# Slots of a state-space stage dealt out anew, and side work held back while loads are played

## The chip, the cores and the metric

The kernel runs on one core of one Trainium2 chip. The metric is the device time of one execution in microseconds (us), the median of several. A core has five engines with instruction streams of their own: TensorE (PE, with its weight loads shown as PEld), VectorE (DVE), ScalarE (ACT), GpSimd (POOL) and SyncE (SP), which here only issues DMAs. 16 DMA engines carry out what SP and POOL issue.

## What is computed

Two layers of an encoder trunk on 256 tokens of width 2048, in float32. Cut to what matters:

```
h = rms_norm(x, norm_mix_g[layer])
...
x = x + mixer_conv_diff(h, ...)      # layer 0: GLU, conv, differential attention
x = x + mixer_s5(h, ...)             # layer 1: state-space layer
...
x = x + memory_cross_attention(rms_norm(x, ..), rms_norm(mem, ..), wq, wk, wv, wo)
x = x + conv_ffn(rms_norm(x, ..), w_up, dw, db, w_down)
...
# mixer_s5, per direction
bu = einsum("sgc,gpc->sgp", u, bb)   # bb from discretised parameters
h  = associative_scan(a, bu)         # over the 256 tokens, 128 groups, 64 states
y  = einsum("sgp,gcp->sgc", h, c)    # both directions summed
...
g = gelu(y + d_skip * xn);  out = (g @ w_val) * sigmoid(g @ w_gate)
```

## The kernel before

**Weights.** Every product with a weight matrix goes through tiles of 128 x 1024 float32 (512 KB), 960 in all. `wtile` (L212) loads one on SP's queue (`raw`, L217, four buffers), casts it on ScalarE to a reduced high part (`hi`, L223), and subtracts on VectorE to get the low part (`lo`, L225); `lin_ws` (L263, L264) and `lin_xs` (L298) multiply high by high, high by low and low by high. The stages follow one another: GLU and attention projections, attention, output projection (`ab_w_out`), cross-attention (`xa_wq`, `xa_wo`), FFN up and down, the state-space layer, cross-attention and FFN of layer 1. The order of the instructions on each engine is fixed when the kernel is built, by a scheduler with its own model of time; on the chip each engine works through its row in that order, and waits where a buffer or an operand isn't there.

**Side work.** What the state-space layer needs of its parameters (W1, W2, the tables d_t) is computed in pieces during layer 0. Generators stand in `self.side`; after each weight tile `background` (L228) adds the stage's rate (`RATE`, L32) to a credit and plays pieces until it is used up. `s5_w1` makes W1 in 32 blocks of 512 KB: for each, six VectorE operations on 128 x 512 (L865, 0.6 credits each), a load on SP (L873, s_b) and eight on POOL (L872, d_pw) into one of two buffers, and a write on SP (L892, d_w). The load for the block after next goes into the buffer that is being written, so it waits in SP's queue for that write. `self.loads` holds loads that are played one per weight tile (`load_one`, L573): the residual x in the first GLU tiles, and before each pair of attention heads of cross-attention their keys and values (`kvraw`, L578), which share the buffers of `raw` and are split by a cast on ScalarE (L310) and a subtraction on VectorE (L311).

**The state-space stage.** `s5` works in large slots named A0, A1, B0, B1 and B2. At its start the residual X is written to DRAM (d_x, L999) as FFN down finishes it, and read back rearranged (xc, L1003, slot A1). `rr` (L1035) holds each token's norm, xg = xc * rr * gain (L1039, eight VectorE operations) goes to B1, and TensorE transposes it (L1045, ps_u) to U in B0. Then eight blocks follow: products of U with a block of W1 (L1058, ps_sa; W1's blocks come in quads, w1s, 2 MB in four loads on POOL, L1022, here numbered 0 to 7, so that W1's second block is block 1), transposes of the result (L1069, ps_st), copies to the state (st). The matrix products of the memory's values and keys for layer 1 (`mem_kv(1)`, weights xa_wv and xa_wk) are set among all this as filling for TensorE. The scans, the state history (hprev), the products with W2 (w2r, on POOL, L1118) and tables (tq, L1120), and gT follow in the same slots.

Of the kernel before, what the change touches and what calls it, by code (L numbers as in the profile page):

```python
# [12 lines left out]
F32 = mybir.dt.float32  # L13
F32R = mybir.dt.float32r
# [8 lines left out]
NTOK = 256  # L23
# [5 lines left out]
RMS_EPS = 1e-6  # L29
LN_EPS = 1e-5  # L30
MAGIC = 12582912.0
RATE = {"glu": 1.2, "qkv": 1.29, "kv": 0.95, "out": 0.8, "wq": .7, "wo": .8, "up": .75, "down": 0.96}  # L32


class Build:
# [177 lines left out]
    def wtile(self, src):  # L213
        nc = self.nc
        part = lambda t: t.rearrange("p (k f) -> p k f", k=src.shape[1])
        raw = part(self.W.tile([128, 1024], F32, tag="raw", name="raw", bufs=4))
        dma = (nc.sync if self.begun else nc.scalar).dma_start(raw, src)  # L217
        self.begun = True
        if self.loads:
            with self.tc.issue_after(dma.ins):  # L220
                self.load_one()
        hi = part(self.W.tile([128, 1024], F32R, tag="hi", name="hi"))
        nc.scalar.copy(hi, raw)  # L223
        lo = part(self.W.tile([128, 1024], F32R, tag="lo", name="lo"))
        ins = nc.vector.tensor_tensor(lo, raw, hi.bitcast(F32), op=ALU.subtract)  # L225
        self.background(ins.ins, dma.ins)
        return hi, lo

    def background(self, ins, dma):
# [129 lines left out]
    def mixer0(self):  # L359
# [10 lines left out]

        self.rate = RATE["glu"]
        self.side.append(self.s5_params())
# [48 lines left out]

        self.rate = RATE["qkv"]
        av = S.tile([128, 2, 2048], F32, tag="B0", name="av")
# [72 lines left out]

        self.rate = RATE["kv"]
        self.side.append(self.s5_w1())
# [7 lines left out]
        cat = lambda kt: (bo[:, 0, kt], bo[:, 1, kt]) if kt < 8 else (ao[:, 0, kt - 8], ao[:, 1, kt - 8])  # L506
        self.rate = RATE["out"]
        w = a["ab_w_out"]
# [73 lines left out]
    def xattn(self, layer):  # L582
# [5 lines left out]
        ov = lambda kt, j: oT[kt // 8][:, j, kt % 8, :]  # L588
        self.rate = RATE["wq"]

# [7 lines left out]
        for h in range(XH):  # L598
# [35 lines left out]
            if h < 2:  # L634
                self.load_head(h + 2)
        self.rate = RATE["wo"]
        for n in range(4):
# [373 lines left out]
    def s5(self):  # L1011
        nc, a, M, S, R = self.nc, self.a, self.M, self.S, self.R
# [4 lines left out]
        quads = []  # L1017

        def load_quad(b):
            t = S.tile([128, 4, 4, 256], F32, tag=("A0", "B2", "A0", "B2", "B1", "B2", "B1", "B2")[b], name="w1s")  # L1020
            for i in range(4):
                nc.gpsimd.dma_start(t[:, i], self.d_w1[b * 4 + i].rearrange("p g r d -> p g (r d)"))  # L1022
            quads.append(t)

        for b in range(2):
            load_quad(b)
        xc = S.tile([128, 8, 512], F32, tag="A1", name="xc")
        self.fetch_xc(xc)
        rr = M.tile([128, 8], F32, name="rr")
# [7 lines left out]
        gc = lambda ap: ap.rearrange("p (g c) -> p g c", c=16)  # L1037
        for t in range(8):
            nc.vector.scalar_tensor_tensor(xg[:, :, 7 - t, :], gc(xc[:, t]), rr[:, t : t + 1], gc(gq), op0=ALU.mult, op1=ALU.mult)  # L1039
        U = S.tile([128, 32, 128], F32, tag="B0", name="U")  # L1040
        for b in range(8):
            ps = self.pst("ps_u")
            for i in range(4):
                gi = b * 4 + i
                nc.tensor.transpose(ps[:, i * 128 : i * 128 + 128], xg[:, gi], self.ident)  # L1045
            (nc.scalar.copy if b % 2 else nc.vector.tensor_copy)(U[:, b * 4 : b * 4 + 4], ps.rearrange("p (i x) -> p i x", i=4))
        self.dump("U", U)
        ST = []
        for b in range(8):
            hf = b // 4  # L1050
            if b % 4 == 0:
                st = S.tile([128, 2, 32, 64], F32, tag=f"A{1 - hf}", name="st")
                ST.append(st)
            pss = [self.pst("ps_sa") for _ in range(2)]
            for i in range(4):
                gi = b * 4 + i
                for q in range(4):
                    nc.tensor.matmul(pss[i // 2][q * 32 : q * 32 + 32, i % 2 * 256 : i % 2 * 256 + 256], lhsT=U[:, gi, q * 32 : q * 32 + 32], rhs=quads[b][:, i, q, :], start=True, stop=True, tile_position=(0, q * 32))  # L1058
            if b < 6:
                load_quad(b + 2)  # L1060
            for h in range(2):
                g2 = b % 4 * 2 + h
                sb = M.tile([128, 2, 512], F32, tag="y", name="sb", bufs=2)[:, 0]
                nc.scalar.copy(sb, pss[h])
                p2 = self.pst("ps_st")
                for i in range(2):
                    for j in range(2):
                        o = j * 256 + i * 128
                        nc.tensor.transpose(p2[:, o : o + 128], sb[:, i * 256 + j * 128 : i * 256 + j * 128 + 128], self.ident)  # L1069
                s4 = p2.rearrange("p (r g k) -> p r g k", r=2, g=8)  # L1070
                d4 = st[:, :, :, g2 * 8 : g2 * 8 + 8].rearrange("p r k g -> p r g k")
                nc.vector.tensor_copy(d4[0:64], s4[0:64])
                nc.scalar.copy(d4[64:128, :, :, ::-1], s4[64:128])
        ring = S.tile([128, 4, 1024], F32, tag="B2", name="w2r")
        gT, hps = [], []

        def scan(hf):
            st = ST[hf]
            gs = slice(hf * 64, hf * 64 + 64)
            Ar = self.A8[:, 0:1, gs].broadcast_to([128, 2, 64])  # L1080
            Ai = self.A8[:, 1:3, gs]
            for k in range(1, 32):
                m1 = M.tile([128, 2, 64], F32, tag="m1", name="m1", bufs=2)
                m2 = M.tile([128, 2, 64], F32, tag="m2", name="m2", bufs=2)
                nc.vector.tensor_tensor(m1, Ar, st[:, :, k - 1, :], op=ALU.mult)
                nc.vector.tensor_tensor(m2, Ai, st[:, ::-1, k - 1, :], op=ALU.mult)
                nc.vector.tensor_tensor(m1, m1, m2, op=ALU.add)
                nc.vector.tensor_tensor(st[:, :, k, :], st[:, :, k, :], m1, op=ALU.add)
            self.dump(f"st{hf}", st)
            hp = S.tile([128, 2, 64, 32], F32, tag=f"B{1 + hf}", name="hprev")  # L1090
            nc.vector.memset(hp[0:64, :, :, 0:1], 0.0)
            nc.vector.memset(hp[64:128, :, :, 31:32], 0.0)
            for g in (slice(0, 16), slice(16, 32), slice(32, 64)):
                for j in range(2):
                    hv = st[:, j, :, g].rearrange("p k g -> p g k")
                    nc.scalar.copy(hp[0:64, j, g, 1:32], hv[0:64, :, 0:31])
                    nc.vector.tensor_copy(hp[64:128, j, g, 0:31], hv[64:128, :, 30::-1])
            hps.append(hp)

        def outside(hf):  # L1100
            hp = hps[hf]
            gt = S.tile([128, 2, 2, 4, NTOK], F32R, tag=f"A{1 - hf}", name="gT")
            gT.append(gt)
            if hf:
                late = S.tile([128, 4, 1024], F32, tag="B1", name="w2r")
                more = [S.tile([128, 2, 1024], F32, tag=f"x2{i}", name="w2r") for i in range(4)]
                slots = [late[:, i] for i in range(4)] + [more[i // 2][:, i % 2] for i in range(8)]
            else:
                slots = [ring[:, i] for i in range(4)]
            for g8 in range(2):  # L1110
                yt = M.tile([128, 8, 8, 16], F32, tag="y", name="yt", bufs=2)
                for b in range(2):
                    ps = self.pst("ps_y")
                    for i in range(4):
# [8 lines left out]
                        for q in range(4):  # L1123
                            nc.tensor.matmul(o[q], lhsT=U[:, gi, q * 32 : q * 32 + 32], rhs=tt[:, :, q, :], start=True, stop=False, tile_position=(0, q * 32))  # L1124
                        for j in range(2):
# [4 lines left out]
                for t4 in range(2):  # L1130
# [5 lines left out]
                    for q in range(4):  # L1136
                        nc.scalar.copy(tv(0)[:, q], s4[:, q])
                        nc.vector.tensor_tensor(tv(1)[:, q], s4[:, q], tv(0)[:, q].bitcast(F32), op=ALU.subtract)

        scan(0)  # L1140
        outside(0)
        scan(1)
        self.mem_kv(1)
        outside(1)
        kts = list(range(16))
        gx = lambda kt: (gT[kt // 8][:, 0, (kt % 8) // 4, kt % 4], gT[kt // 8][:, 1, (kt % 8) // 4, kt % 4])
# [122 lines left out]
```

## Time and profile before

| what | value |
|---|---|
| median of 3 runs | 2898.45 us (2898.27 to 2898.61) |
| profiled execution | 2897.15 us |
| its span in the trace | 2895.0 us |
| TensorE busy | 2854.1 us |
| VectorE, ScalarE, GpSimd busy | 2203.7, 1492.3, 265.3 us |
| weight tiles | 960 of 512 KB |
| DMA over the span | 678.34 MB, 234 GB/s |

The span is what the trace covers; the execution's own time has 2.15 us around it. Busy time is the time in which an engine worked on an instruction. A view by stretches gives each engine's busy time and number of instructions between two moments of the span; a view of waits names for an engine what ended its idle time, in total us, times and longest; a timeline lists instructions with the idle time before them and what released them in brackets, like rows next to each other put together. SPq and POOLq are the queues of DMA issues of these engines.

### The profile page before, as it was taken

What the parts mean: (1) busy time and instruction counts of PE and PEld (TensorE: products, weight loads), DVE (VectorE), ACT (ScalarE), POOL (GpSimd) and SP (SyncE); (2) the same over time, 40 slices, a digit from 0 to 9 for tenths busy, and PEclk for the clock granted to TensorE, in tenths of its full rate; (3) what the DMA queues carried; (4) which work ended last, traced back from release to release, by engine and by line L of the source; (5) the groups of instructions that cost most, each with busy time, mean ns of one, the idle gap of its engine ahead of it and who ended that gap; (6) DMA issues with size and microseconds to landing.
All of it is one profiled execution on the core that took longest, in us unless ns stands there. A gap on an engine that the chain in (4) does not pass through costs nothing. (4 is left out here: it accounts for less than half of the span.)

```text
span 2895.0 us, 44267 instructions
## 1 busy us (share of the span) xinstructions
PE 2854.1 (99%) x16673; PEld 2411.6 (83%) x16673; DVE 2203.7 (76%) x3524; ACT 1492.3 (52%) x2015; POOL 265.3 (9%) x504
## 2 busy tenths in 40 slices
PE   8999999999999999999999999999999999999998
PEld 7888887888888888888886787788888888888887
DVE  8899987877899887889855994556567776467765
ACT  6455554454555543455544544555455555345543
POOL 1000112222210102020201021000000000000000
PEclk9999999999999999999999999999999999999999
DMA  8655669978986788777887787655455555555554
GB/s 292 230 176 195 203 223 320 300 247 286 300 298 233 243 276 267 250 256 233 281 286 282 271 338 273 211 189 182 163 193 193 189 190 190 195 189 189 187 192 160
DMA packets 207143, 678.34 MB, mean 234 GB/s; under 512 B 33521, under 2 KB 36337, under 8 KB 206417
## 3 DMA queue, kind: packets, MB, share of 16 engines
q1 hardware_dynamic: 178592, 598.17, 61.1%
q0 software_dynamic: 28192, 76.83, 8.0%
q8 instruction: 130, 2.13, 0.3%
q14 instruction: 85, 0.69, 0.1%
q10 hardware_dynamic: 144, 0.52, 0.1%
HBM read 624.67 MB, written 61.08 MB: 237 GB/s over the span
## 5 line engine op out<-in xcount | busy, mean ns | idle before, releaser
L225 DVE TENSOR_TENSOR lo<-raw,hi 128x1024 fp32r<-128x1024 f32 x960 | 1173.1, 1223 | 534.6 <-ACT hi L223 530.9
L223 ACT CAST hi<-raw 128x1024 fp32r<-128x1024 f32 x960 | 1008.5, 1051 | 964.4 <-PE ps_xs L298 429.0
L263 PE MATMUL ps_ws<-x,hi 128*128 128x512 f32 x4352 | 1350.7, 396 | 8.0 <-DVE x L177 7.4
L264 PEld LDWEIGHTS ps_ws<-x,lo 128*128 128x128 f32 x4352 | 793.3, 188 | 191.4 <-DVE lo L225 14.8
L264 PE MATMUL ps_ws<-x,lo 128*128 128x256 f32 x4352 | 846.2, 280 | 8.1 <-DVE lo L225 7.7
L263 PEld LDWEIGHTS ps_ws<-x,hi 128*128 128x128 f32 x4352 | 674.3, 189 | 21.9 <-DVE x L177 7.4
L298 PE MATMUL ps_xs<-hi,hb 128*128 128x512 f32 x1328 | 356.5, 389 | 0.0
L298 PEld LDWEIGHTS ps_xs<-hi,hb 128*128 128x128 f32 x1328 | 249.1, 188 | 51.8
L298 PE MATMUL ps_xs<-lo,hb 128*128 128x512 f32 x664 | 204.8, 390 | 0.0
L298 PE MATMUL ps_xs<-hi,x 128*128 128x512 f32 x640 | 177.3, 394 | 1.9 <-ACT hi L223 1.9
L872 POOL DMA_DIRECT2D w1s<-d_pw x256 | 122.4, 486 | 589.5 <-DVE w1s L865 271.6
L298 PEld LDWEIGHTS ps_xs<-lo,hb 128*128 128x128 f32 x664 | 124.4, 188 | 25.9
L298 PEld LDWEIGHTS ps_xs<-hi,x 128*128 128x128 f32 x640 | 119.1, 188 | 31.6 <-issue 5.5
L298 PE MATMUL ps_xs<-hi,oT 128*128 128x512 f32 x512 | 141.1, 392 | 0.8 <-ACT hi L223 0.8
L298 PE MATMUL ps_xs<-hi,gT 128*128 128x512 f32 x512 | 138.1, 391 | 0.3 <-ACT hi L223 0.3
L271 ACT COPY z<-ps_ws 128x512 f32<-128x512 f32 x88 | 51.6, 587 | 145.2 <-PE ps_ws L263 145.2
L298 PEld LDWEIGHTS ps_xs<-hi,gT 128*128 128x128 f32 x512 | 95.6, 188 | 21.1 <-issue 0.8
L676 ACT ACTIVATE c<-z,fdb,fdw 128x256 f32<-128x256 f32 x176 | 96.3, 595 | 30.5 <-DVE z L671 30.4
L298 PEld LDWEIGHTS ps_xs<-hi,oT 128*128 128x128 f32 x512 | 95.3, 188 | 20.1 <-ACT hi L223 1.0
L529 DVE SCALAR_TENSOR_TENSOR av<-hpt,cdw,av 128x256 f32<-128x256 f32 x240 | 109.9, 484 | 0.7
L272 DVE TENSOR_TENSOR z<-ps_ws,z 128x512 f32<-128x512 f32 x88 | 60.7, 690 | 56.0 <-ACT z L271 55.7
L298 PE MATMUL ps_xs<-lo,x 128*128 128x512 f32 x320 | 100.8, 394 | 0.0
(288 smaller groups left out, 2582.0 us busy)
## 6 DMA issues: line engine op xcount, KB each, us to landing
raw<-ffn_w_up SPq DMA_DIRECT2D x352, 512.0 KB, 3.6
raw<-ffn_w_down SPq DMA_DIRECT2D x176, 512.0 KB, 4.3
raw<-xa_wv SPq DMA_DIRECT2D x64, 512.0 KB, 4.1
raw<-xa_wk SPq DMA_DIRECT2D x64, 512.0 KB, 4.4
raw<-xa_wq SPq DMA_DIRECT2D x64, 512.0 KB, 4.3
raw<-xa_wo SPq DMA_DIRECT2D x64, 512.0 KB, 3.7
raw<-ab_w_in SPq DMA_DIRECT2D x63, 512.0 KB, 3.7
w1s<-d_pw POOLq DMA_DIRECT2D x256, 64.0 KB, 5.4
```

What stands on the lines that cost most here:

```text
L223: nc.scalar.copy(hi, raw)
L225: ins = nc.vector.tensor_tensor(lo, raw, hi.bitcast(F32), op=ALU.subtract)
L263: both = lambda c: nc.tensor.matmul(ps[:, c], lhsT=hi[:, kk, sl[c]], rhs=x2, start=first, stop=last)
L264: low = lambda c: nc.tensor.matmul(ps[:, c, 1], lhsT=lo[:, kk, sl[c]], rhs=xh, start=False, stop=False)
L271: self.nc.scalar.copy(out, ps[:, :, 1])
L272: self.nc.vector.tensor_tensor(out, ps[:, :, 0], out, op=ALU.add)
L298: ins = mm()
L529: nc.vector.scalar_tensor_tensor(ac[:, ct, :], hp[:, ct, j : j + NTOK], cdw[:, ct, j : j + 1], ac[:, ct, :], op0=ALU.mult, op1=ALU.add)
L676: nc.scalar.activation(c[:, i], zt[:, i, 1 : NTOK + 1], AF.Identity, bias=fdb[:, ft : ft + 1], scale=w(1))
L872: nc.gpsimd.dma_start(pw[t * 16 : t * 16 + 16], self.d_pw[t, k * 4 : k * 4 + 4].partition_broadcast(16))
```

## The change

It has three parts. First, `wtile` remembers whether it has played a load (`busy`); if so, this tile adds no credit and plays no side work. Second, the rates of three stages: output projection 0.8 to 0.5, query projection 0.7 to 0.75, FFN up 0.75 to 0.8. Third, slots of `s5`: W1's eight blocks take A0, A1, B1, A0, A1, B1, A1, B1 in place of A0, B2, A0, B2, B1, B2, B1, B2; the second is loaded into A1, which held xc, after xg has read it, the third after the transposes to U into B1, which held xg; later ones three blocks ahead, the last two two blocks ahead. States, hprev, gT and the rings of W2 get the slots left. The loop over a block's four parts runs from the last to the first.

```
-RATE = {"glu": 1.2, "qkv": 1.29, "kv": 0.95, "out": 0.8, "wq": .7, "wo": .8, "up": .75, "down": 0.96}
+RATE = {"glu": 1.2, "qkv": 1.29, "kv": 0.95, "out": 0.5, "wq": .75, "wo": .8, "up": .8, "down": 0.96}
...
-        if self.loads:
+        busy = bool(self.loads)
+        if busy:
             with self.tc.issue_after(dma.ins):
                 self.load_one()
...
-        self.background(ins.ins, dma.ins)
+        if not busy:
+            self.background(ins.ins, dma.ins)
...
-            t = S.tile([128, 4, 4, 256], F32, tag=("A0", "B2", "A0", "B2", "B1", "B2", "B1", "B2")[b], name="w1s")
+            t = S.tile([128, 4, 4, 256], F32, tag=("A0", "A1", "B1", "A0", "A1", "B1", "A1", "B1")[b], name="w1s")
...
-        for b in range(2):
-            load_quad(b)
+        load_quad(0)
         xc = S.tile([128, 8, 512], F32, tag="A1", name="xc")
...
             nc.vector.scalar_tensor_tensor(xg[:, :, 7 - t, :], gc(xc[:, t]), rr[:, t : t + 1], gc(gq), op0=ALU.mult, op1=ALU.mult)
+        load_quad(1)
...
+        load_quad(2)
         ST = []
...
-                st = S.tile([128, 2, 32, 64], F32, tag=f"A{1 - hf}", name="st")
+                st = S.tile([128, 2, 32, 64], F32, tag=("B2", "A0")[hf], name="st")
...
-            for i in range(4):
+            for i in range(3, -1, -1):
...
-            if b < 6:
+            if b < 3:
+                load_quad(b + 3)
+            elif 4 <= b < 6:
                 load_quad(b + 2)
...
-        ring = S.tile([128, 4, 1024], F32, tag="B2", name="w2r")
+        ring = S.tile([128, 4, 1024], F32, tag="B1", name="w2r")
...
-            hp = S.tile([128, 2, 64, 32], F32, tag=f"B{1 + hf}", name="hprev")
+            hp = S.tile([128, 2, 64, 32], F32, tag=("A1", "B1")[hf], name="hprev")
...
-            gt = S.tile([128, 2, 2, 4, NTOK], F32R, tag=f"A{1 - hf}", name="gT")
+            gt = S.tile([128, 2, 2, 4, NTOK], F32R, tag=("B2", "A0")[hf], name="gT")
...
-                late = S.tile([128, 4, 1024], F32, tag="B1", name="w2r")
+                late = S.tile([128, 4, 1024], F32, tag="A1", name="w2r")
```

SP's row in the output projection, around its four loads of keys and values (kvraw). d_w<-w1s is the write of a W1 block, w1s<-s_b the load that follows into the buffer. Before:

```order
L873 DMA w1s<-s_b 128x1024
L217 DMA raw<-ab_w_out 128x1024 x2
L892 DMA d_w_87<-w1s 128x1024
L578 DMA kvraw<-d_kT_2968 128x1024
L217 DMA raw<-ab_w_out 128x1024
L873 DMA w1s<-s_b 128x1024
L578 DMA kvraw<-d_v_2969 128x2x512
L217 DMA raw<-ab_w_out 128x1024
L578 DMA kvraw<-d_kT_2968 128x1024
L217 DMA raw<-ab_w_out 128x1024
L892 DMA d_w_87<-w1s 128x1024
L578 DMA kvraw<-d_v_2969 128x2x512
```

The same place in the changed kernel:

```order
L217 DMA raw<-ab_w_out 128x1024 x5
L580 DMA kvraw<-d_kT_2968 128x1024
L894 DMA d_w_87<-w1s 128x1024
L217 DMA raw<-ab_w_out 128x1024
L875 DMA w1s<-s_b 128x1024
L580 DMA kvraw<-d_v_2969 128x2x512
L217 DMA raw<-ab_w_out 128x1024
L580 DMA kvraw<-d_kT_2968 128x1024
L217 DMA raw<-ab_w_out 128x1024
L580 DMA kvraw<-d_v_2969 128x2x512
L217 DMA raw<-ab_w_out 128x1024 x9
```

The first pair of write and reload stands between the first two loads in both; the write next to the fourth load is gone, and nine weight loads follow without one. Counted by stage, W1's writes on SP were 7 in the output projection, 6 with `xa_wq`, 7 with `xa_wo` and 9 in FFN up; they are 4, 6, 7 and 12. In the query projection the write and the reload that stood by the second pair of loads now stand by the first: the row is write, kvraw, reload, weight tile, kvraw.

POOL's row at the start of the state-space stage (w1s with its number is one block of W1, tq and d_t are the tables, w2r is W2). Before:

```order
L1120 DMA tq_15413<-d_t_90 128x512
L1022 DMA w1s_14749<-d_w1_87 128x1024 x4
L1022 DMA w1s_14926<-d_w1_87 128x1024 x4
L1022 DMA w1s_14844<-d_w1_87 128x1024 x4
L1022 DMA w1s_14885<-d_w1_87 128x1024 x4
L1022 DMA w1s_14967<-d_w1_87 128x1024 x4
```

In the changed kernel:

```order
L1125 DMA tq_15413<-d_t_90 128x512
L991 DMA d_t_90<-d_g_91 128x1x512 x8
L1024 DMA w1s_14771<-d_w1_87 128x1024 x4
L1024 DMA w1s_14825<-d_w1_87 128x1024 x4
L1024 DMA w1s_14849<-d_w1_87 128x1024 x4
L1024 DMA w1s_14890<-d_w1_87 128x1024 x4
```

W1's second block (w1s_14749, now w1s_14771) is still the first in this row, but it now waits for xg to have read its slot, and the others follow it in order; block 4 (w1s_14926) stood ahead of block 2. The last eight table writes (d_t) have moved behind the first five table loads. In SP's row the reading of xc has moved ahead of one weight load: two of them stood between d_x and xc, now there is one.

TensorE's row around blocks 3 to 5 (ps_sa are their products, 16 instructions a block, which the trace counts as 32; ps_st the transposes; ps_xs the memory projection). Before:

```order
L1058 MATMUL ps_sa<-w1s,U 32x256 x4
L1069 MATMUL ps_st<-ident,sb 128x128 x4
L1058 MATMUL ps_sa<-w1s,U 32x256 x8
L298 MATMUL ps_xs<-hi,x_13853 128x512 x4
L298 MATMUL ps_xs<-lo,x_13853 128x512 x2
L298 MATMUL ps_xs<-hi,x_13853 128x512 x4
L298 MATMUL ps_xs<-lo,x_13853 128x512 x2
L298 MATMUL ps_xs<-hi,x_13853 128x512 x4
L298 MATMUL ps_xs<-lo,x_13853 128x512 x2
L1069 MATMUL ps_st<-ident,sb 128x128 x4
L1058 MATMUL ps_sa<-w1s,U 32x256 x8
```

In the changed kernel:

```order
L1074 MATMUL ps_st<-ident,sb 128x128 x8
L1061 MATMUL ps_sa<-w1s,U 32x256 x16
L300 MATMUL ps_xs<-hi,x_13885 128x512 x2
L300 MATMUL ps_xs<-lo,x_13885 128x512 x2
L300 MATMUL ps_xs<-hi,x_13885 128x512 x2
L300 MATMUL ps_xs<-hi,x_13846 128x512 x2
L300 MATMUL ps_xs<-lo,x_13846 128x512 x2
L300 MATMUL ps_xs<-hi,x_13846 128x512 x4
```

A block's products, cut in pieces of 4 and 8 before, stand in one piece of 16 in blocks 0 to 5 of the changed kernel and in two pieces of 8 in the last two: 20 pieces before, 10 now.

## Prediction

> **What bounds the kernel now.** I read the page first, then the matrix engine's busy time by stretches, then what its feeders waited for in the stretches that aren't full, and last the timeline of the one stretch that is nearly half empty. From the page:
>
> ```profile
> span 2895.0 us, 44267 instructions
> PE 2854.1 (99%) x16673; PEld 2411.6 (83%) x16673; DVE 2203.7 (76%) x3524; ACT 1492.3 (52%) x2015; POOL 265.3 (9%) x504
> L225 DVE TENSOR_TENSOR lo<-raw,hi 128x1024 fp32r<-128x1024 f32 x960 | 1173.1, 1223 | 534.6 <-ACT hi L223 530.9
> ```
>
> TensorE is the bound: 2854.1 of 2895.0 us. All that an edit of queues can win is the idle 41 us, and what TensorE does slowly. Each of 960 weight tiles goes through a load, a cast on ScalarE and a subtraction of 1.22 us on VectorE, in order, so a late tile shows as idle time of TensorE. The stretches that the change touches in layer 0 (columns: stretch, its length, busy time and count of PE, PEld, DVE, ACT, POOL, then the granted clock, DMA share, GB/s):
>
> ```profile
> 480.00:500.00 20.00, 18.55 (x85) 14.78 (x84) 15.15 (x20) 10.21 (x17) 7.18 (x16) 1.00 0.91 288
> 500.00:520.00 20.00, 16.57 (x71) 11.89 (x70) 17.60 (x23) 11.45 (x17) 3.81 (x8) 1.00 0.94 304
> 520.00:540.00 20.00, 19.84 (x91) 15.81 (x90) 14.50 (x21) 9.71 (x15) 3.83 (x8) 1.00 1.00 312
> 600.00:620.00 20.00, 16.54 (x97) 13.33 (x95) 13.88 (x20) 9.77 (x15) 3.82 (x8) 1.00 0.73 230
> ```
>
> In the output projection (480 to 540) 1.45 + 3.43 + 0.16 = 5.0 us are idle, in the query projection (600 to 620) 3.5 us. Both hold the loads of keys and values (kvraw), which share SP's queue and ScalarE's order with the weights. ScalarE's wait at 480 to 520, SP's waits at 470 to 640 (total, times, longest), and SP's timeline:
>
> ```profile
> ACT kT L310 <- DMA kvraw<-d_kT: 8.1, 2, 6.5
> SPq L873 <- DMA d_w<-w1s: 36.9, 10, 6.5
> 483.88 0.33 SPq L217 DMA_DIRECT2D raw<-ab_w_out  x1
> 488.73 0.33 SPq L873 DMA_DIRECT2D w1s<-s_b  x1
> 489.16 0.53 SPq L578 DMA_DIRECT2D kvraw<-d_v  x1
> 493.38 0.33 SPq L217 DMA_DIRECT2D raw<-ab_w_out  x1
> ```
>
> SP waits at L873, before it may reload a W1 buffer, until the write of its former content (d_w) has landed: 36.9 us in 10 waits. Everything behind stands still; two weight loads are 9.5 us apart here. The next large hole is the start of the state-space stage:
>
> ```profile
> 1520.00:1530.00 10.00, 10.00 (x48) 8.30 (x47) 4.84 (x12) 3.16 (x3) 0.00 (x0) 1.00 1.05 347
> 1530.00:1540.00 10.00, 5.80 (x24) 3.96 (x22) 5.50 (x9) 3.14 (x3) 0.00 (x0) 0.84 0.45 153
> 1540.00:1550.00 10.00, 10.00 (x53) 8.97 (x54) 5.86 (x7) 5.12 (x8) 0.00 (x0) 0.82 0.59 211
> 1590.00:1600.00 10.00, 9.46 (x68) 6.17 (x67) 8.38 (x20) 7.01 (x8) 4.02 (x8) 1.00 1.03 413
> 1740.00:1750.00 10.00, 7.92 (x99) 6.24 (x98) 5.68 (x9) 7.70 (x7) 4.21 (x9) 1.00 0.67 261
> ```
>
> 4.2 us idle at 1530 to 1540, with the clock down to 0.84 and 0.82, right after a stretch in which the DMA engines were full (1.05). Its timeline:
>
> ```profile
> 1514.97 2.09 POOL L1022 DMA_DIRECT2D w1s<-d_w  x4 [55.11 <-PE ps_xs L298]
> 1515.43 0.93 SPq L999 DMA_DIRECT2D d_x<-X  x2
> 1524.28 0.33 SPq L1003 DMA_DIRECT2D xc<-d_x  x1
> 1529.06 0.16 DVE L1035 COPY rr<-ps_rr 128x8 f32<-128x8 f32 x1
> 1532.53 1.05 ACT L223 CAST hi<-raw 128x1024 fp32r<-128x1024 f32 x1 [4.64 <-DMA raw<-xa_wv]
> 1534.50 5.39 DVE L1039 SCALAR_TENSOR_TENSOR xg<-xc,rr,gq 128x512 f32<-128x512 f32 x8 [5.28 <-DMA xc<-d_x]
> 1536.58 1.08 PE L298 MATMUL ps_xs<-hi,x 128*128 128x512 f32 x2 [1.91 <-ACT hi L223]
> 1539.94 3.68 PE L1045 MATMUL ps_u<-ident,xg 128*128 128x128 f32 x16 [2.29 <-DVE xg L1039]
> 1549.23 1.04 PE L1045 MATMUL ps_u<-ident,xg 128*128 128x128 f32 x8
> ```
>
> W1's second block (2 MB, four loads on POOL at 1514.97) is issued half a microsecond ahead of the last write of the residual (d_x, 1515.43). The residual must come back as xc; xc was issued at 1524.28 and xg began at 1534.50. Weights are late in the same stretch (ScalarE waited 4.64 us). TensorE idled 1.91 us for a tile and 2.29 us for xg, and the first 16 transposes took 3.68 us where 8 later took 1.04.
>
> **The change part by part.** The sum is made against the profiled execution, 2897.15 us, which lies 1.3 us under the median of 2898.45. About 0.2% (5.8 us) is what a measurement of this kernel can tell from no change.
>
> *Output projection* (rate 0.8 to 0.5, and no side work in a tile that plays a load). By SP's order two of the four loads there had a pair of W1's write and reload next to them; now the first alone has. The nearest row for loads with no side work at all is the same helper in layer 1's GLU projection:
>
> ```profile
> 1840.00:1860.00 20.00, 19.55 (x87) 15.89 (x86) 9.53 (x8) 8.94 (x10) 0.00 (x0) 1.00 0.60 194
> 1860.00:1880.00 20.00, 18.87 (x86) 15.11 (x86) 15.28 (x18) 12.90 (x20) 0.00 (x0) 1.00 0.79 266
> ```
>
> They leave 0.45 + 1.13 = 1.6 us idle. So at best all 5.0 us go, at worst none, and I take 5.0 - 1.6 = **-3.4**.
>
> *Query projection.* Before, the second pair of loads stood around a W1 pair and cost the 3.5 us; now the second is free of it, and the first has W1's write, kvraw, W1's reload, the next tile and kvraw in a row. If position in the queue decides, the hole only moves (0); if the empty tile decides, it goes (-3.5). I take the half, **-1.7**.
>
> *Start of the state-space stage.* W1's second block now takes the slot of xc and is issued behind xg, so that d_x, xc and the weights have the DMA engines to themselves. Its cost without that load, from the same transfers at quieter times (medians at 1420 to 1512, issue to landing):
>
> ```profile
> d_x<-X SPq DMA_DIRECT2D x6, 256.0 KB, 5.7
> xc<-d_x SPq DMA_DIRECT2D x3, 512.0 KB, 7.7
> ```
>
> 1515.43 + 5.7 + 7.7 = 1528.8; rr is there at 1529.06; xg takes 5.39, to 1534.5. TensorE without its idle 4.2 us would reach the transposes at 1539.94 - 4.2 = 1535.7, so nothing is left to wait for. The slow clock goes with the hole: 3.68 - 2 x 1.04 = 1.6 us. All of it is 5.8. If d_x is no quicker, xc lands at 1524.28 + 7.7 = 1532.0, xg ends at 1537.4, and 1.7 us stay; if xc is no quicker either, nothing is won. I take **-5.5**, bounds 0 and -5.8. SP's order also has xc one weight tile earlier.
>
> *The eight blocks of W1.* By TensorE's order the products (ps_sa) of the eight blocks stood in 20 pieces among tiles of the memory projection; now they stand in 10, blocks 0 to 5 whole. The price of a cut, from an uncut block and a quarter of one:
>
> ```profile
> 1561.01 1.93 PE L1058 MATMUL ps_sa<-w1s,U 128*32 128x256 f32 x32
> 1590.33 0.64 PE L1058 MATMUL ps_sa<-w1s,U 128*32 128x256 f32 x8
> ```
>
> 0.64 - 1.93 / 4 = 0.16 us for each, so ten fewer are -1.6 at most, and nothing if the neighbours overlap; I take three quarters, **-1.2**. The wait for a block at 1590 to 1600 (0.54 idle) I leave as it is, since the loop now begins with the part that lands last. Moving W1's second block past xg on POOL delays the six blocks behind it by nothing, as they wait for slots; the load of the state-space tables' last part (d_t), now behind the first five tq loads in that queue, is read by later tq loads only: 0. States, hprev, gT and the W2 ring change slots with each other; no row prices that, the nearest hole in their part is the 2.1 us at 1740 to 1750, so I take 0 with 2 to either side. What hides the blocks' transfers:
>
> ```profile
> w1s<-d_w POOLq DMA_DIRECT2D x24, 512.0 KB, 9.7
> 1535.00:1615.00 80.00, 75.50 (x523) 51.72 (x524) 52.87 (x89) 45.30 (x54) 12.51 (x24) 0.96 0.76 284
> ```
>
> 80 us at 284 GB/s are 22.7 MB; with the second block 24.8 MB. At the 413 GB/s of the full stretch at 1590 above that takes 60 us, and some 73 are there: cover of 13 us. The Trainium skill ("SBUF — State Buffer", Summary) wants end-to-end times of HBM transfers estimated at about 358 GB/s. By that 24.8 MB would take 69 us and the cover would shrink to 4 us, so the sum would lose some of its gain to late blocks; the rows with 413 GB/s speak for the larger cover.
>
> *FFN up of layer 0* (rate 0.75 to 0.8, and three more W1 blocks, 12 for 9). The stretch before, the subtractions in it, and one side operation in VectorE's durations (least, median, most, in ns):
>
> ```profile
> 780.00:1035.00 255.00, 255.00 (x1683) 222.09 (x1682) 242.54 (x371) 141.76 (x186) 32.13 (x56) 1.00 0.79 266
> 780.00:1035.00 255.00, 108.58 (x89) 1.00 0.79 266
> L865 DVE TENSOR_TENSOR w1s<-w1s x104: 679/685/694, 472.0 to 853.5; 128x512 f32<-128x512 f32 x104
> ```
>
> VectorE is 95% busy and hides all of it: TensorE has 255.00 of 255. A tile takes 255 / 89 = 2.87 us; 0.05 more credit at 0.6 an operation is 0.083 operations a tile, 0.06 us, or 89 x 0.06 = 5 us: 97%. It fits as an average, not at every place. I take **+1** (0 to +5, all of it uncovered). What left the first GLU tiles and the residual's loads lies beside full TensorE: 0.
>
> Sum: -3.4 - 1.7 - 5.5 - 1.2 + 1 = -10.8, thus 2897.15 - 10.8 + 1.3 = 2887.65; I forecast **2887.5 us**. With all bounds on the good side it is 2898.45 - 5.0 - 3.5 - 5.8 - 1.6 - 2 = 2880.5.
>
> **The rivals.**
>
> *Nothing at the state-space start* (0.18). The chain write, read, multiply is serial, and six weight loads stand with xc in SP's queue; if these and not W1's block fill the DMA engines, xg starts as late. For it: the d_x and xc medians come from loaded stretches too. Against: W1's 2 MB are the one thing new there, and DMA is at 1.05 just then. It gives -10.8 + 5.5 = -5.3: 2893.1 us, no change.
>
> *Slower: W1's chain in FFN up* (0.10). Six operations at 0.6 per block are 3.6 credits, at rate 0.8 a block each 4.5 tiles, 12.9 us. In that time its buffer must be written and refilled (medians of the transfers at 470 to 1040):
>
> ```profile
> d_w<-w1s SPq DMA_DIRECT2D x27, 512.0 KB, 6.5
> w1s<-s_b SPq DMA_DIRECT2D x25, 512.0 KB, 4.1
> ```
>
> 6.5 + 4.1 = 10.6 us, so 2.3 us are spare. From 12.9 us on, VectorE stops at the side operation and the tile's subtraction behind it is late, and SP holds the weights. Each microsecond over is paid in 12 blocks: 2 us over give 24 us, 2911.5 us. Against it: the output projection ran at 0.8 before, and its 520 to 540 lost 0.16 us only.
>
> *Late W1 blocks* (0.10). The tail has two slots, and each block is used from its last part on. Blocks 1 and 5 began 29.3 us apart (1561.01 and 1590.33), 7.3 us a block, so two blocks ahead are 14.6 us, against 9.7 for one load and, for the last of the four, up to the 5.1 us more that 2.1 MB take at 413 GB/s: 14.8. Late by 1 to 1.5 us in blocks 4 to 7, it costs 4 to 6 us: 2891.5 to 2893.5. The Trainium skill ("DMA: Bandwidth & Descriptors", Rules for kernel authors) says to issue a transfer early and to wait for it late; the change issues W1's second block some 20 us later. By that rule this rival is the likely one; before, that block was issued 46 us ahead of its use (1514.97 and 1561.01), and the trace shows what that cost the transfers beside it.
>
> *The side work does not leave the loads* (0.05). One W1 pair is still next to a load in each projection; if that one pair makes the whole hole, out and query keep their 5.1 us: 2892.6.
>
> **How the numbers follow.** The forecast has 0.57; its own range is 2880 to 2892. The rest are the four cases. The range goes from 2880 to 2900 (state-space start, late blocks and the moved slots together: 2887.5 + 5.5 + 5 + 2); only the slow rival lies beyond. Faster by over 0.2% is below 2892.65: the forecast, half of the two last cases and a few of the first, 0.68. Within 0.2%: 0.21. Slower: 0.11.
>
> **What would show it.** Right: at 1520 to 1550 PE is full, its clock 1.00, POOL's second block is issued behind xg, and the first 16 transposes take about 2.1 us; 480 to 520 holds under 2 us idle; FFN up stays full. Wrong: SP's wait at W1's reload in FFN up with idle PE; PE waiting for w1s in blocks 4 to 7; xg still started by xc later than 1532.

## The result, and the profile after

The changed kernel takes 2884.66 us (median of 6 runs, 2878.82 to 2889.12) against 2898.53 us before (6 runs, 2897.01 to 2901.63): a ratio of 0.995, 95% interval 0.9938 to 0.9962, some 14 us faster. The forecast was 2887.5, some 11 us. The profiled execution took 2884.62 us, its span is 2882.8.

The page of the changed kernel, first its two top lines:

```profile
span 2882.8 us, 44251 instructions
PE 2852.0 (99%) x16673; PEld 2414.3 (84%) x16673; DVE 2200.3 (76%) x3524; ACT 1492.6 (52%) x2015; POOL 265.0 (9%) x504
```

The span is 12.2 us shorter. TensorE's busy time fell by 2.1 us, so 10.1 us are idle time that is gone. Where, the busy time by stretches tells; these are the stretches of layer 0 that were shown of before, and FFN up (second column the length, then PE's busy time; the last but one is the DMA share):

```profile
480.00:500.00 20.00, 19.60 (x90) 15.50 (x88) 13.61 (x18) 10.65 (x16) 3.50 (x8) 1.00 0.81 264
500.00:520.00 20.00, 18.95 (x84) 14.81 (x83) 16.99 (x21) 12.60 (x19) 3.81 (x8) 1.00 0.80 256
520.00:540.00 20.00, 20.00 (x94) 16.62 (x93) 14.01 (x19) 10.17 (x15) 3.81 (x8) 1.00 0.85 294
600.00:620.00 20.00, 19.44 (x122) 17.07 (x121) 17.38 (x25) 11.03 (x16) 2.39 (x5) 1.00 0.73 234
780.00:1035.00 255.00, 252.32 (x1656) 218.33 (x1655) 244.49 (x375) 140.46 (x183) 36.24 (x69) 1.00 0.81 269
```

The output projection's idle time fell from 5.0 to 1.5 us, and the DMA share with it, from 0.91, 0.94 and 1.00 to 0.81, 0.80 and 0.85. The query projection's hole fell from 3.5 to 0.6. FFN up, full before, now idles 2.7 us. The start of the state-space stage, by stretches and in the timeline:

```profile
1520.00:1530.00 10.00, 10.00 (x47) 8.32 (x46) 8.33 (x12) 3.27 (x4) 0.12 (x1) 1.00 0.61 209
1530.00:1540.00 10.00, 10.00 (x62) 8.76 (x61) 6.53 (x8) 6.07 (x9) 2.87 (x6) 1.00 0.89 320
1540.00:1550.00 10.00, 10.00 (x73) 7.33 (x71) 4.09 (x5) 3.66 (x5) 3.38 (x7) 1.00 1.02 388
1740.00:1750.00 10.00, 9.57 (x75) 7.50 (x76) 2.37 (x2) 2.70 (x3) 2.21 (x5) 1.00 1.03 412
1750.00:1780.00 30.00, 27.09 (x281) 21.61 (x280) 9.39 (x15) 10.17 (x17) 3.15 (x6) 0.94 0.68 265
```

```profile
1512.20 0.33 SPq L1001 DMA_DIRECT2D d_x<-X  x1
1515.54 0.32 SPq L1005 DMA_DIRECT2D xc<-d_x  x1
1524.19 5.39 DVE L1040 SCALAR_TENSOR_TENSOR xg<-xc,rr,gq 128x512 f32<-128x512 f32 x8
1529.88 2.19 POOL L1024 DMA_DIRECT2D w1s<-d_w  x4 [68.69 <-DVE xg L1040]
1531.15 1.91 PE L1047 MATMUL ps_u<-ident,xg 128*128 128x128 f32 x16
```

xc is issued 3.3 us behind the last d_x (8.3 before, where the second of the two d_x was issued at 1516.03), xg starts 8.7 us behind xc (10.2 before), W1's block 1 follows xg, and the 16 transposes take 1.91 us, not 3.68, at a clock of 1.00. TensorE waits for nothing here. The stage's end lost ground: at 1740 to 1780 TensorE idles 3.3 us with the DMA engines full at first (1.03), and the clock is down to 0.94 at 1750 to 1780; before, 2.1 us were idle at 1740 to 1750, and the clock stayed at 1.00. The waits there (total, times, longest):

```profile
POOL w2r L1123 <- PE ps_ws L265: 7.5, 4, 2.2
POOL tq L1125 <- DMA w2r<-d_w: 6.2, 4, 2.0
PE ps_y L1129 <- DMA tq<-d_t: 2.9, 2, 2.0
```

TensorE now waits for the tables tq, which are issued behind loads of W2, which wait for slots that the memory projection frees late.

### The profile page after: what moved, and what is told of

It reads as the page before. It is cut to its first block, busy times and chain, and to the rows that moved or that the text cites. A ratio compares the mean times of both kernels' runs of the same rounds, so it can differ in the third digit from the quotient of the medians.

```text
span 2882.8 us, 44251 instructions
## 1 busy us (share of the span) xinstructions
PE 2852.0 (99%) x16673; PEld 2414.3 (84%) x16673; DVE 2200.3 (76%) x3524; ACT 1492.6 (52%) x2015; POOL 265.0 (9%) x504
## 4 chain that ended last, share of the span: by engine, by line
PE 92%; DMA 4%; DVE 2%; ACT 1%; issue 1%; SPq 0%; ACTq 0%; DVEq 0%; POOL 0%; POOLq 0%
PE ps_xs L300 37%; PE ps_ws L265 32%; PE ps_ws L266 16%; DVE lo L226 1%; PE ps_e L300 1%; ACT hi L224 1%; DMA d_w<-w1s 1%; PE ps_k L967 1%; PE ps_sa L1061 1%; DMA w2r<-d_w 1%; DMA raw<-xa_wq 0%; DMA tq<-d_t 0%; PE ps_xt L158 0%; DMA raw<-ffn_w_up 0%; PE ps_s L457 0%
```

## The experiments

Twelve kernels were run. One table first: idle time of TensorE in us by stretch, from the profiled execution of each (length less busy time), and the median's ratio to the kernel before on the same chip with its interval. Before and after are for comparison.

| kernel | 0:440 | 440:560 | 560:640 | 640:765 | 765:1035 | 1500:1600 | 1720:1800 | ratio |
|---|---|---|---|---|---|---|---|---|
| before | 11.2 | 5.1 | 3.7 | 1.2 | 0.0 | 4.8 | 2.3 | |
| after | 9.2 | 1.5 | 0.6 | 1.1 | 2.7 | 0.0 | 3.6 | 0.995 [0.9938, 0.9962] |
| e1_rates_only | 8.9 | 3.5 | 0.5 | 2.1 | 5.5 | 4.2 | 2.1 | 0.9993 [0.9982, 1.0003] |
| e2_slots_only | 11.0 | 5.4 | 3.1 | 1.2 | 0.0 | 0.0 | 4.1 | 0.9973 [0.9963, 0.9982] |
| e3_late_load | 11.4 | 5.0 | 2.2 | 1.2 | 0.0 | 0.0 | 2.3 | 0.9977 [0.9967, 0.9986] |
| e8_dummy | 9.1 | 1.4 | 0.5 | 1.1 | 5.3 | 3.1 | 1.3 | 0.9962 [0.995, 0.9974] |
| e4_sb_pool | 12.3 | 7.0 | 4.9 | 1.2 | 0.0 | 3.4 | 2.4 | 1.0 [0.9989, 1.0011] |
| e12_no_reload | 11.7 | 0.4 | 0.3 | 1.2 | 0.0 | 4.2 | 2.3 | 0.9945 [0.9932, 0.9958] |
| e13_no_arith | 14.8 | 20.0 | 1.7 | 0.0 | 0.0 | 3.5 | 2.1 | 1.0109 [1.0093, 1.0125] |
| e9_busy_only | 9.1 | 5.2 | 3.6 | 1.2 | 0.4 | 0.0 | 3.9 | 0.9977 [0.9968, 0.9986] |
| e5_after_sb_pool | 9.3 | 5.5 | 0.1 | 1.1 | 1.1 | 0.0 | 3.2 | 0.9955 [0.994, 0.997] |
| e6_up75 | 9.1 | 2.1 | 1.7 | 1.1 | 3.1 | 0.0 | 3.5 | 0.9949 [0.9932, 0.9965] |
| e14_pool_late | 8.9 | 3.4 | 2.2 | 4.6 | 7.8 | 0.0 | 4.0 | 0.9956 [0.9943, 0.9969] |
| e11_tq_sp | 9.0 | 1.8 | 0.0 | 1.1 | 5.7 | 0.0 | 3.7 | 0.9959 [0.9944, 0.9973] |

After, e8 and e11 have the same edits in layer 0, and yet FFN up idles 2.7, 5.3 and 5.7 us: one execution's idle time there is good to some 3 us only.

**The two halves of the change.** The first takes the rates and the rule of the tile with a load, the second the slots.

```
# e1: the kernel before, with
RATE "out" 0.5, "wq" .75, "up" .8;  if not busy: self.background(...)
# e2: the changed kernel, with the RATE of before, and self.background(...) always
```

> The first two parts of the change alone (rates, and no side work in a tile that plays a load); the state-space stage with the slots of before. If the gains of layer 0 come from these two parts and not from the slots: idle time of TensorE at 440 to 640 falls from about 9 us to about 2, FFN up of layer 0 has some 2.7 us idle, the state-space start keeps its 4.2 us hole and its slow clock; span about 2895.0 - 5 = 2890. If the slots were the whole gain: no less than 2893.

> The slots of the state-space stage alone, with the rates and the side work of before. If the parts are independent: layer 0 as before to a few tenths, including its 5 us and 3.5 us holes and a full FFN up; the start of the state-space stage without its hole; span about 2895.0 - 8 = 2887. If the stage's gain depended on side work having ended at another time: some of the hole at 1530 stays, span over 2890.

Measured: 2895.24 and 2891.89 us, with 2899.05 before. The halves are independent in place: e1 keeps the hole at 1530 and e2 keeps those of layer 0. In e1, 2.3 us are won up to 440, 1.6 in the output and 3.2 in the query projection, and 5.5 are lost again in FFN up; its interval holds no change. Its profiled execution was its longest, with a span of 2900.7 against some 2890 expected; its runs lie between 2889.86 and 2902.51. The slots alone are worth 7.8 us (0.27%); e2's span was 2890.4 against 2887 expected, in an execution whose clock fell to 0.96 at 440 to 560.

**What made the start of the state-space stage late.** One kernel takes the crowding out of the old layout, the other puts it into the new.

```
# e3: the kernel before, with
-        for b in range(2):
-            load_quad(b)
+        load_quad(0)
...
+        gate = S.tile([128, 4, 4, 256], F32, tag="B2", name="gate")
+        nc.vector.tensor_copy(gate[:, 0, 0, 0:1], xg[:, 0, 7, 0:1])
+        load_quad(1)
# e8: the changed kernel, with
         load_quad(0)
+        spare = S.tile([128, 4, 4, 256], F32, tag="B2", name="spare")
+        for i in range(4):
+            nc.gpsimd.dma_start(spare[:, i], self.d_w1[4 + i].rearrange("p g r d -> p g (r d)"))
```

> The kernel before, with one thing changed: W1's block 1 is issued only after xg, in its old slot B2 (a copy of one column to that slot, behind xg on VectorE, makes it wait). Crowding (the 2 MB ahead of d_x and xc were the cause): the hole at 1530 to 1540 and the slow clock go, about 5.8 us, span about 2889. Serial chain (the way of the residual through DRAM is slow by itself): no change, 2895. Block 1 too late for its use at 1561: a new wait of TensorE for w1s there, up to 3 us.

> The changed kernel, with 2 MB of W1 loaded once more, for no use, at the place where block 1 was loaded before (POOL, ahead of xc, into the free slot B2). Crowding: xc lands late again and the hole at the start of the stage comes back, 4 to 6 us, span about 2888. Serial chain or slots: no hole, span 2883 to 2884.

The timeline of e3, then that of e8:

```profile
1517.94 0.32 SPq L1003 DMA_DIRECT2D xc<-d_x  x1
1526.59 5.39 DVE L1038 SCALAR_TENSOR_TENSOR xg<-xc,rr,gq 128x512 f32<-128x512 f32 x8
1533.55 1.91 PE L1047 MATMUL ps_u<-ident,xg 128*128 128x128 f32 x16
```

```profile
1514.27 2.19 POOL L1030 DMA_DIRECT2D spare<-d_w  x4 [49.53 <-PE ps_xs L300]
1522.64 0.33 SPq L1005 DMA_DIRECT2D xc<-d_x  x1
1532.39 5.39 DVE L1043 SCALAR_TENSOR_TENSOR xg<-xc,rr,gq 128x512 f32<-128x512 f32 x8 [4.77 <-DMA xc<-d_x]
1537.84 3.68 PE L1050 MATMUL ps_u<-ident,xg 128*128 128x128 f32 x16 [2.59 <-DVE xg L1043]
```

With block 1 late, in its old slot, the hole is gone and the transposes take 1.91 us; with 2 MB that nobody needs in its old place, the hole is back (3.1 us, less than the 4 to 6 expected), the transposes take 3.68 us and xg waits for xc. The transfers themselves show it: from issue to landing the last d_x took 8.2 us and xc 10.1 before, 7.3 and 9.6 in e8, but 3.3 and 6.7 in after and 3.3 and 5.4 in e3. xc's place among SP's weight loads changed too (one weight load ahead of it in e3 as in after, two in e8 as before), but in all four traces xc is issued within 0.1 us of the landing of d_x, so its place held nothing up. Crowding is shown from both sides; the serial way through DRAM is not the cause. No product waited for block 1. The sizes: in e3 the stage shortened by 5.8 us (from the 508th to the 636th weight cast on ScalarE: it was 1.4 us ahead of before at its start, 7.2 at its end), the whole kernel to 0.9977, 6.7 us. In e8, against after, 6.1 us were lost up to the 572nd cast (it had won 12.2 us in after and 6.1 in e8 since the stage began), and 4.0 came back behind it: the tail's waits (3.6 us at 1720 to 1800, 1.3 in e8) and the slow clock that they bring (some 1.7 us in after, none in e8) are not reached when TensorE comes later. So the stage's end hides a part of what its start wins. By the medians e8's loss against after is not clear of the noise (0.9962 and 0.995, with intervals that overlap); it shows in the traces.

**What made the holes of the output and query projections late.** The prediction read SP's wait at the reload of W1 as the cause.

```
# e4: the kernel before, with
-            nc.sync.dma_start(b.rearrange("p g c d -> p (g c d)"), a["s5_b1"][k])
+            nc.gpsimd.dma_start(b.rearrange("p g c d -> p (g c d)"), a["s5_b1"][k])
# e12: the kernel before, with
-            if k < 31:
+            if k < 1:
                 load(k + 1)
# e13: the kernel before, without the six tt(...) of s5_w1
# e9: the changed kernel, with the RATE of before
```

> The kernel before, with one thing changed: the reload of a W1 buffer (s_b) is issued on POOL in place of SP, so that SP no longer stands still for the write ahead of it; rates, side work and slots as before. If SP's wait is what makes the holes of the output and query projections: idle time of TensorE at 440 to 640 falls from about 9 us to 2 or 3, span about 2889. If the holes come from the side work's bytes, or from the casts of keys and values in ScalarE's order: idle time there within 2 us of before, span 2893 to 2896.

> The kernel before without the loads of W1's side work from the third block on (its arithmetic runs on what the buffers hold, its writes stay): it leaves out two thirds of the side work's transfers, and SP's waits for them, and keeps VectorE's work. If full DMA engines make the holes of the output and query projections: idle time at 440 to 640 falls from about 9 us to 3 or less, and the DMA share there from 0.9 and more to about 0.7. If VectorE's and ScalarE's work per tile makes them: 7 us or more stay.

> The kernel before without the arithmetic of W1's side work (its six VectorE operations a block are left out; loads and writes stay, at the same tiles). If full DMA engines make the holes: idle time at 440 to 640 stays at 7 us or more. If VectorE's work per tile makes them: 3 us or less, with the DMA share as before.

> The changed kernel with the three rates of before: only the rule that a tile which plays a load plays no side work, and the slots. If that rule is what empties the holes of the output and query projections: idle time at 440 to 640 about 2 us, as in the changed kernel, and FFN up full or nearly so: span 2880 to 2882. If the lower rate of the output projection is what does it: 5 us or more idle at 440 to 640, span 2885 or more.

The stretch of the output projection, one row each, in the order before, e4, e12, e13, e9:

```profile
440.00:560.00 120.00, 114.86 (x535) 92.44 (x535) 95.88 (x130) 56.07 (x76) 34.34 (x72) 1.00 0.97 317
```

```profile
440.00:560.00 120.00, 113.03 (x525) 90.44 (x524) 96.14 (x125) 56.21 (x76) 39.11 (x80) 1.00 0.96 308
```

```profile
440.00:560.00 120.00, 119.57 (x582) 100.25 (x581) 105.11 (x148) 60.64 (x82) 0.00 (x0) 1.00 0.74 244
```

```profile
440.00:560.00 120.00, 100.02 (x394) 74.14 (x392) 50.04 (x52) 41.58 (x52) 62.81 (x130) 0.90 1.04 282
```

```profile
440.00:560.00 120.00, 114.80 (x539) 93.03 (x539) 94.78 (x127) 57.57 (x77) 30.50 (x64) 1.00 0.92 306
```

The theory of SP's wait falls. In e4 SP waits no more for a write to land, and its row has the four loads without a pair between them; yet two weight loads are 10.1 us apart, as far as the 9.5 us of before:

```profile
486.69 0.33 SPq L217 DMA_DIRECT2D raw<-ab_w_out  x1
496.81 0.34 SPq L217 DMA_DIRECT2D raw<-ab_w_out  x1
```

The holes are as large as before or larger (7.0 and 4.9 us), with the DMA engines as full, 0.96. The move had a price of its own, as VectorE stood 8.3 us for operands of W1's side work at 440 to 560 (5.3 before); but 5.2 of the 7.0 us lie at 480 to 520, where no such wait was longer than 0.3 us. In e12 W1's arithmetic stays, and VectorE is busier than before (105.1 of 120 us), but most transfers are gone: 0.4 and 0.3 us idle, DMA share 0.74. It leaves out SP's waits at the reload too, but e4 shows that those alone change nothing. ScalarE, which stood up to 6.5 us before a cast of keys or values (6.9 in e4), stands 2.3 us there at most. In e13 the arithmetic is gone and the transfers stay; unpaced by it they bunched together, the share rose to 1.04 and 20 us were idle, with VectorE half idle. That is more than expected of the side of the transfers, and it shows them without VectorE. So late transfers on full DMA engines make the hole of the output projection: a tile with a load wants 1 MB in place of 512 KB, and side work with its blocks of 1.5 MB was laid on top.

For the query projection the row of 20 us does not show it (its share is 0.73 before and after); rows of 5 us of before do, where the weights are late:

```profile
610.00:615.00 5.00, 3.44 (x20) 2.64 (x19) 3.21 (x5) 2.36 (x6) 1.94 (x5) 1.00 0.97 254
615.00:620.00 5.00, 4.41 (x25) 3.08 (x23) 3.30 (x5) 2.88 (x4) 0.00 (x0) 1.00 1.00 347
```

The other 1.3 of its 3.5 us are a wait for the queries (qT), at 602.6.

e9 tells what the rule does without the lower rate. In the output projection 5.2 us stay, so it takes the rate, which moves the transfers out; the rate without the rule was not run. In the query projection the rule empties 600 to 620, but 3.6 us appear in a new place, at the first pair of loads:

```profile
600.00:620.00 20.00, 20.00 (x125) 17.84 (x124) 14.12 (x20) 11.17 (x16) 0.00 (x0) 1.00 0.68 237
577.61 0.58 PE L596 MATMUL ps_xs<-kT,qT 128*128 128x256 f32 x1 [3.60 <-ACT qT L312]
```

With the rates as well they are gone; which rate does it is not told apart. The rule alone wins the 2 us before 440.

**What made FFN up late.**

```
# e6: the changed kernel, with RATE "up" .75
# e5: the changed kernel, with the reload on POOL, as e4
# e14: the changed kernel, with
+            (nc.gpsimd if self.rate == RATE["up"] else nc.sync).dma_start(...)
```

> The changed kernel with the rate of FFN up back at 0.75. If the rate made FFN up late: it is full again, span about 2880. If the number of W1 blocks that were pushed into FFN up matters and not their pace: it still idles 2 us or more, span 2882 to 2883.

> The changed kernel, with the reload of a W1 buffer (s_b) issued on POOL. If SP's wait at that reload is what made FFN up of layer 0 lose 3.5 us: TensorE idles less than 0.5 us there, and the rest of layer 0 is no worse, span about 2879. If VectorE's load at the higher rate is the cause: FFN up keeps 2 us or more of idle time, span 2882.

> The changed kernel, with the reload of a W1 buffer on POOL in the cross-attention's output projection and in FFN up only (the two stages with rate 0.8), on SP elsewhere. If SP's wait at the reload makes FFN up late, as the run with all reloads on POOL showed: FFN up loses under 1.5 us, the earlier stages are as in the changed kernel, span 2877 to 2881, and the median 3 to 5 us under the changed kernel's. If the gain is lost to the tail, which waits for its transfers: span 2881 or more.

FFN up of e6 and of e5, and waits of e14 at 815 to 836:

```profile
765.00:1035.00 270.00, 266.94 (x1685) 231.44 (x1684) 258.29 (x390) 147.78 (x192) 32.21 (x67) 1.00 0.81 267
```

```profile
765.00:1035.00 270.00, 268.86 (x1759) 233.72 (x1758) 260.11 (x401) 149.25 (x194) 43.63 (x85) 1.00 0.83 273
```

```profile
DVE w1t L867 <- DMA w1s<-d_pw: 9.2, 1, 9.2
POOL w1s L874 <- DMA w1s<-s_b: 7.4, 1, 7.4
PE ps_ws L266 <- DVE lo L226: 6.6, 1, 6.6
```

The pace alone is not the cause: at 0.75 FFN up idles 3.1 us. SP's waits at the reload there (total, times, longest) grew from before to after:

```profile
SPq L873 <- DMA d_w<-w1s: 24.2, 6, 5.1
SPq L875 <- DMA d_w<-w1s: 45.8, 9, 6.6
```

With the reload off SP's queue FFN up idles 1.1 us, and nothing before 900, with 12 W1 writes as in the changed kernel, VectorE as busy, and the DMA engines as full (shares of 0.91 and 0.93 at 780 to 820, against 0.84 and 0.97). So here SP's wait seems to be what costs; but it is one execution of e5, against 2.7 to 5.7 us in executions with the same rates and the reload on SP. And POOL is no better place: e14 moved the reload for two stages only, and in its profiled execution VectorE stopped 9.2 us at a side operation whose operands POOL had issued late, the subtraction behind it was late and TensorE lost 6.6 us in one piece. e5 has a like stop, smaller, in its output projection, where it makes 2.1 of the 5.5 us:

```profile
451.63 0.69 DVE L867 TENSOR_TENSOR w1t<-w1s 128x512 f32<-128x512 f32 x1 [3.98 <-DMA w1s<-d_pw]
453.51 0.73 PE L300 MATMUL ps_xs<-lo,bo 128*128 128x512 f32 x2 [2.08 <-DVE lo L226]
```

That is the stop which the slow rival of the prediction foretold, though from POOL's late issue and not from the rate; in the changed kernel's profile VectorE has none in FFN up. e14's executions lie between 2878.44 and 2899.78 us, so whether it is any better stays open. The spans of all three missed what was expected (2885.6, 2886.0 and 2898.0, against 2877 to 2883).

**What the tail waits for.**

```
# e11: the changed kernel, with
-                        nc.gpsimd.dma_start(tq, self.d_t[gi])
+                        (nc.sync if hf else nc.gpsimd).dma_start(tq, self.d_t[gi])
```

> The changed kernel with the second half's table loads (tq) issued on SP, where they don't stand behind W2's loads. It tells what makes TensorE wait for tq near 1760. If POOL's row does (a table load behind W2 loads that wait for slots): those 3.3 us go, span about 2879. If the DMA engines are simply full there: they stay as waits for tq, W2 or weights, span 2882 to 2884.

Waits of e11 at 1728 to 1768:

```profile
PE ps_y L1132 <- DMA w2r<-d_w: 3.7, 2, 3.1
```

The wait for tq went, and a wait for W2 of the same size took its place (3.7 us idle at 1720 to 1800, as after). So POOL's row alone is not the limit. That the transfers are, because they can't begin before the memory projection frees their slots, fits POOL's waits (8.0 us for ps_ws here, 7.5 in after), but no run moved those slots. None of these kernels beats the changed one by more than the intervals (e6 has 0.9949, after 0.995).

## Why the prediction was right, and where its reasons were not

*Start of the state-space stage* (-5.5): right in place, cause and size. 4.2 us idle and 1.8 us of slow transposes are gone in after, 6.0 in all; e3 alone shows 5.8 us. xg ended at 1529.6, not at 1534.5, but 3.8 of these 4.9 us are what layer 0 had won; the chain itself was only about 1 us quicker than the sum had it. (The sum counts from the first of two d_x; the last was issued at 1516.03.) The Trainium skill ("DMA: Bandwidth & Descriptors", Rules for kernel authors) would have transfers issued early; here the early one was the harm, and 46 us of lead bought nothing.

*Output projection* (-3.4): the size was right (-3.6), the cause was not. The step that failed is the one that read SP's wait of 36.9 us as what holds the weights up. It stands on the row of SP's waits and on two weight loads 9.5 us apart; but of the 9.5 us that wait was 4.5, and without it (e4) they were 10.1. What held them up were slow loads on full DMA engines, and the shares of 0.91 to 1.00 stood in the very rows that were quoted. The analog in layer 1 (1.6 us without side work) gave the right size, as it has no transfers of side work at all, whichever way they do harm.

*Query projection* (-1.7): mis-sized, -3.1. The half stood between two cases, the hole moves or the hole goes, and SP's queue was to decide. With the rule alone it did move to the first pair of loads (e9), and with the rates it went; that transfers taken out of the stage before could do this was not considered. And 1.3 of the 3.5 us had not been a wait for weights.

*FFN up* (+1, bound 5): mis-sized; 2.7 in the changed kernel's profile, 5.3 to 5.7 in three other executions with the same rates. VectorE's room, from which the sum was made, is there (244.49 of 255 us); the loss seems to be SP's wait at the reload, which the part on FFN up left to the rival. It is the one of the prediction's own signs of being wrong that came.

*W1's blocks* (-1.2): the stage as a whole lost 8.4 us (the 508th cast came 3.8 us earlier, the 636th 12.2). Idle time accounts for 4.8 + 0.3 - 1.3 = 3.8 (1500 to 1600, 1600 to 1700, 1720 to 1800), the slow clock at the start for 2.3 (the transposes for 1.8, two products ahead of them, with 1.08 us in place of 0.62, for 0.5), and the tail's slow clock takes some 1.7 back. 4.0 are left for less work of TensorE, and most of it lies where the forecast looked, only larger. The products of the eight blocks alone, before and after:

```profile
1500.00:1800.00 300.00, 19.19 (x256) 0.99 0.79 290
1500.00:1800.00 300.00, 15.89 (x256) 0.99 0.80 294
```

They take 3.3 us less for ten pieces fewer, 0.33 us a piece; the estimate of 0.16 us a cut was half of that. No product waited for a block, at up to 409 GB/s in the stretch at 1560 to 1570:

```profile
1550.00:1560.00 10.00, 10.00 (x96) 7.03 (x96) 6.01 (x6) 6.35 (x8) 2.10 (x4) 1.00 1.03 408
1560.00:1570.00 10.00, 10.00 (x72) 7.58 (x73) 4.34 (x4) 6.60 (x9) 2.09 (x4) 1.00 1.03 409
```

So the larger cover held. The figure of about 358 GB/s that the Trainium skill ("SBUF — State Buffer", Summary) wants for estimates was exceeded for 20 us on end.

*What was taken as nothing:* the first 440 us won 2.0 us where 0 was put: 1.3 at 380 to 400, where the cause was not sought, and 0.8 in GLU's first tiles, where the residual's loads are (before, then after):

```profile
20.00:40.00 20.00, 17.67 (x95) 13.68 (x95) 18.27 (x58) 16.77 (x37) 0.00 (x0) 1.00 0.91 333
20.00:40.00 20.00, 18.45 (x103) 15.15 (x103) 14.66 (x37) 18.01 (x39) 0.00 (x0) 1.00 0.97 360
```

Here VectorE got room (18.27 to 14.66 us busy) while the DMA share rose, so this gain is not one of emptier DMA engines. The tail lost 1.3 us of idle time and some 1.7 of slow clock: when the start of the stage comes earlier, the end runs into transfers that seem unable to start earlier.

The errors are -0.2 (output projection), -1.4 (query projection), -0.5 (start), +1.7 (FFN up), -2.1 (blocks, by their products), -0.6 (waits for blocks at 1560 to 1600, left as they were and gone), -2.0 (first 440 us) and +3.0 (tail). With the forecast's -10.8 that is -12.9, and the span shows -12.2. In layer 0 idle time fell by 6.1 us, while the 508th cast came only 3.8 earlier: 2.3 us came back as busy time of TensorE, most of it in FFN up and down, and were not placed; some 1.6 us more were won in the stage. So it is in part luck that the total came near: terms that won 6.8 us more than forecast and terms that lost 4.7 more nearly cancel, and the output projection's size came from an analog and not from its cause. How much of the whole is layer 0's share stays open to some microseconds: e1 alone is worth 2 us (interval -1 to 5), while the changed kernel is 6.7 us better than e2 alone, on intervals of 3 us either way.

## What to carry to other kernels

When an engine's queue waits for a transfer, don't blame the queue's order from its row of waits: moving the wait to another queue costs one line to try, and here it changed nothing in the output projection and, by one execution, most in FFN up. The DMA share alone does not tell the two apart: it was 0.95 at 500 to 520 of e4, 0.97 at 800 to 820 of the changed kernel's FFN up, and the kernel before ran full there at 0.94. Taking the transfers out told it. A load that is needed late is dear when it is issued just ahead of a short chain that is needed at once; tie its issue to the end of that chain. And an earlier start is worth only what the end of the stage can take: find what can't begin earlier there before counting the gain.

## What the hardware showed that was not expected

The same instructions in layer 0 gave 2.7, 5.3 and 5.7 us of idle time in FFN up in three executions (after, e8, e11), and the kernel before took 2890.99 to 2904.84 us over the 27 runs beside the first experiments: a term of 1 or 2 us in such a stage can be forecast as a mean only.

The 16 transposes took 3.68 us where TensorE had just idled 4.2 and 3.1 us (before, e8), and 1.91 us where it had not (after, e3), with granted clocks of 0.84 and 1.00 in the stretch at 1530. In rows of 1 us the clock of before is 0.50 at 1537 to 1543 and 1.00 around that. Such a hole costs about half as much again as its idle time, but not every hole does. The holes of the output projection left the clock at 1.00 before and brought it to 0.96 in e2, which has the same layer 0. And in e4 the transposes behind a wait of 2.60 us ran at a clock of 1.00:

```profile
1543.20 1.97 PE L1045 MATMUL ps_u<-ident,xg 128*128 128x128 f32 x16 [2.60 <-DVE xg L1039]
```

What decides it these runs do not tell.
